# Early distance tables, other places for the dilated tiles, later forget sums and one held gate tile in a hybrid attention layer

## The chip, the cores and the metric

The kernel runs on one core of a Trainium2 chip. It is one launch of a whole decoder layer in float32. The metric is the device time of that launch in microseconds; lower is better. The kernel was run three times and profiled in one more execution.

## What the reference computes

One layer over x of 1024 positions by 1024 channels. Cut to what matters here:

```python
h = rms_norm(x, norm_mix_g)
proj = h @ w_in      # 3*768 dilated q,k,v | 3*512 forgetting q,k,v | 8 forget | 2*1024 gates
for g, (window, dilation) in enumerate(((128, 1), (512, 4), (2048, 16))):
    # 4 heads of 64 each: query t sees t, t-d, ..., t-window, with an ALiBi slope
    outs[g], lses[g] = dilated_window_attention(q[g], k[g], v[g], window, dilation, slopes[g])
o_a = sum(softmax(lses, over g) * outs)              # 256 channels
o_b = forgetting_attention(q, k, v, log_sigmoid(f_logit))   # 8 heads, causal, 512 channels
#   logit[t, s] = q_t.k_s/8 + c_t - c_s, c = cumsum of the log forget gates
x = x + (sigmoid(gate_a) * (o_a @ w_dil_out) + sigmoid(gate_b) * (o_b @ w_fox_out)) @ w_out
h2 = rms_norm(x, norm_ffn_g)
x = x + (silu(h2 @ w_g) * (h2 @ w_u)) @ w_ffn_down    # 2816 hidden channels
return rms_norm(x, norm_final_g)
```

## The kernel before

**How queues are ordered.** The kernel is written as one Python function, and a list scheduler of the framework orders the instructions of every engine when it is built, by a simulated time line; on the chip every engine then works through its queue in that order and waits on semaphores. A pool of tiles takes a place in SBUF when it is opened; a later pool may lie over bytes that an earlier one has given back. An instruction that writes such a tile waits on the chip for the last readers and writers of just those bytes (`reuse_waits="tile"`).

**Arithmetic.** A float32 matmul is made of three: `split` (L94 to 96) takes a tensor apart into a rounded high part, a copy on ScalarE, and the rest, a subtraction on VectorE; `mm3` (L98 to 101) then issues high by high, low by high and high by low. On the profile's rows such groups have the tiles `wh`, `wl` and the like.

**Stages, by their time in the profile.** To about 66 us the input is normed and transposed to `hT`, and the values of the forgetting attention are made. Then come the values of the dilated attention (pool `dilv`, to 140 us): eight row tiles by `w0` (264 columns, the last eight of which are the forget logits `lf`) and eight by `w12` (512 columns), stored by ScalarE's DMA queue to `vd_dram`. `form` (L393 to 418), called twice, makes the tables T1 to T4, sums of quarters of `hT` for a fast block product (seven products in place of eight). The pool `cums` (L451 to 485) makes the running sums of the log forget gates: a triangular matrix `upper` on POOL (GpSimd), a chain of logarithms on VectorE and ScalarE, two matmuls, and the small tile `negc`, which is a bias of the first attention's scores. From there to 270 us, `projections` (L275 to 310) makes q and k of the forgetting attention and four dilated ones, two column tiles in a call, eight calls in all; its weight sums s12 and s34 are made on POOL by `left_side` (L254 to 266). Then the forgetting attention (`fox_qk`, `fox_scores`, `fox_exp`, `fox_values`; 270 to 511 us) and the dilated one (`dil_qk`, `dil_scores`, `dil_exp`, `dil_values`; to 673 us). Both go in units: scores of one unit, then the values of the one before. Each unit has a maximum over partitions on POOL (`partition_all_reduce`).

**Filler.** Two lists are multiplied by `ahead` (L214 to 225) whenever the scheduler finds room on TensorE during both attentions: BESIDE, the eight other tiles of dilated q and k, and `merge_order`, the sixteen tiles of gate logits. One such tile is 48 matmuls of 512 columns into two banks `pf`, two copies by ScalarE into a tile `fst` (two buffers), and a store on ScalarE's DMA queue to `dqk_dram` or `g_dram`. Their pool `ahead` lies on the right side of SBUF, over bytes of the projections' pool (`cc`, `v2`, `v3`).

**Around the dilated attention.** Its pool `dil` holds three distance tables R0 to R2 (L617 to 645; two IOTAs, masks on POOL and VectorE, scratch in the pool `dilm`), then the values `vd` in one tile of 24,576 bytes per partition (three loads on POOL's queue, L647 to 650), then the pool `dila`: six dqk tiles of 4,096 bytes (loads on SP's queue), score tiles L0, L1, L2, the maxima Mx, and `o`. All of it begins at the end of `hT`, at bytes that T and then `vf`, `ql`, `qx`, `kx` and `qraw` of the first attention have held. The scratch of the tables has the bytes 28,160 to 32,256 from there, and so has the first dqk tile.

**Merge.** From 684 us the pool `gates`, at the same first bytes, loads the attention outputs from `o_dram` to `land` tiles (POOL's queue), splits them to `oh` and `ol` (`oh` of the first branch: the first 16,384 bytes), multiplies by the output weights and by the sigmoid of the gates read from `g_dram`. Then follow w_out, the feed-forward's first half (to 1264 us) and second half.

## Time and profile before

| | |
|---|---|
| median of the runs | 1544.46 us (1544.28 to 1544.62) |
| profiled execution, its own time | 1544.29 us |
| span of its instructions | 1542.5 us |
| TensorE clock granted, mean | 0.987 of full speed |
| busy: TensorE, its weight loads, VectorE, ScalarE, GpSimd | 96%, 78%, 58%, 35%, 27% |
| moved by DMA | 171.62 MB, mean 111 GB/s |

Times in the rows are microseconds from the start of the span. PE is TensorE, PEld its weight loads, DVE VectorE, ACT ScalarE, POOL GpSimd, SP SyncE; a name with a q, as SPq, is the part of an engine that issues DMAs. A row names the line, the operation and its tiles as output<-input, with the numbers of buffers left out. The busy time of an engine does not count waiting.

### The profile page before, as it was taken

What the parts mean: (1) busy time and instruction counts of PE and PEld (TensorE: products, weight loads), DVE (VectorE), ACT (ScalarE), POOL (GpSimd) and SP (SyncE); (2) the same over time, 40 slices, a digit from 0 to 9 for tenths busy, and PEclk for the clock granted to TensorE, in tenths of its full rate; (3) what the DMA queues carried; (4) which work ended last, traced back from release to release, by engine and by line L of the source; (5) the groups of instructions that cost most, each with busy time, mean ns of one, the idle gap of its engine ahead of it and who ended that gap; (6) DMA issues with size and microseconds to landing.
All of it is one profiled execution on the core that took longest, in us unless ns stands there. A gap on an engine that the chain in (4) does not pass through costs nothing.

```text
span 1542.5 us, 18138 instructions
## 1 busy us (share of the span) xinstructions
PE 1478.9 (96%) x6956; PEld 1196.4 (78%) x6956; DVE 895.5 (58%) x1321; ACT 536.0 (35%) x808; POOL 419.1 (27%) x351
## 2 busy tenths in 40 slices
PE   7998999799999999979999999999999999999997
PEld 6898888676767777758888778888878877788886
DVE  6741433299997289846727864444444445956546
ACT  5321222376665123335414332222222224312113
POOL 1001331263452111100000145555555553140000
PEclk9999999999999999989999999999999999999999
DMA  7231333743332651145713122222222225642302
GB/s 219 71 101 48 95 109 110 218 109 106 99 103 69 209 181 55 55 163 185 265 56 136 42 69 82 82 82 82 83 82 82 82 88 195 204 140 82 96 15 96
DMA packets 139047, 171.62 MB, mean 111 GB/s; under 512 B 6992, under 2 KB 108368, under 8 KB 138960
## 3 DMA queue, kind: packets, MB, share of 16 engines
q1 hardware_dynamic: 119824, 112.25, 24.4%
q0 software_dynamic: 9616, 34.62, 6.1%
q10 hardware_dynamic: 9520, 23.60, 4.1%
q8 instruction: 55, 0.90, 0.2%
q14 instruction: 32, 0.26, 0.1%
HBM read 123.25 MB, written 47.19 MB: 110 GB/s over the span
## 4 chain that ended last, share of the span: by engine, by line
PE 79%; DMA 6%; DVE 4%; POOL 4%; ACT 3%; issue 2%; SPq 1%; ACTq 0%; POOLq 0%; DVEq 0%
PE pd L272 25%; PE pd L100 10%; PE pd L101 10%; PE pd L99 10%; PE pf L101 4%; PE pf L100 4%; PE pf L99 4%; DMA wr<-in_w_ffn_in_dram 2%; ACT wh L95 2%; PE pd L189 2%; PE pd L190 2%; PE pd L193 2%; PE pd L589 2%; POOL sg L969 1%; DVE wl L96 1%
## 5 line engine op out<-in xcount | busy, mean ns | idle before, releaser
L95 ACT ACTIVATE wh<-wr 128x1024 fp32r<-128x1024 f32 (+2 forms) x152 | 140.6, 932 | 342.8 <-PE pd L100 92.7
L96 DVE TENSOR_TENSOR wl<-wr,wh 128x1024 fp32r<-128x1024 f32 (+2 forms) x152 | 166.9, 1102 | 143.7 <-ACT wh L95 143.4
L272 PE MATMUL pd<-hT_t,wh 128*128 128x512 f32 x784 | 244.7, 393 | 3.0 <-ACT c L952 2.3
L272 PE MATMUL pd<-tT,wh 128*128 128x512 f32 x672 | 206.4, 389 | 0.9 <-DVE v L884 0.6
L272 PEld LDWEIGHTS pd<-hT_t,wh 128*128 128x128 f32 x784 | 148.3, 190 | 34.5 <-ACT c L952 2.7
L99 PE MATMUL pf<-hT_t,wh 128*128 128x512 f32 x384 | 151.7, 395 | 8.0 <-ACT fst L224 7.8
L272 PE MATMUL pd<-hT_t,wl 128*128 128x512 f32 x392 | 155.0, 396 | 1.5 <-DVE wl L96 1.1
L100 PE MATMUL pf<-hT_t,wh 128*128 128x512 f32 x384 | 151.9, 396 | 0.0
L101 PE MATMUL pf<-hT_t,wl 128*128 128x512 f32 x384 | 151.6, 395 | 0.0
L272 PEld LDWEIGHTS pd<-tT,wh 128*128 128x128 f32 x672 | 126.0, 188 | 27.9 <-DVE v L884 1.1
L99 PE MATMUL pd<-wh,wh 128*128 128x512 f32 x352 | 137.4, 391 | 4.4 <-DVE acc L1012 3.1
L100 PE MATMUL pd<-wl,wh 128*128 128x512 f32 x352 | 137.0, 389 | 0.0
L101 PE MATMUL pd<-wh,wl 128*128 128x512 f32 x352 | 137.0, 389 | 0.0
L272 PE MATMUL pd<-tT,wl 128*128 128x512 f32 x336 | 129.7, 389 | 0.2 <-DVE wl L96 0.2
L1012 DVE TENSOR_TENSOR acc<-pd,acc 128x512 f32<-128x512 f32 x128 | 85.8, 688 | 68.2 <-PE pd L101 68.1
L259 POOL TENSOR_TENSOR s<-wr 128x512 f32<-128x512 f32 x26 | 36.6, 1409 | 293.7 <-DVE tT L96 192.4
L96 DVE TENSOR_TENSOR wl<-s,wh 128x1024 fp32r<-128x1024 f32 x52 | 64.8, 1246 | 67.8 <-ACT wh L95 67.8
L95 ACT ACTIVATE wh<-s 128x1024 fp32r<-128x1024 f32 x52 | 55.1, 1060 | 131.4 <-POOL s L260 98.4
L99 PEld LDWEIGHTS pf<-hT_t,wh 128*128 128x128 f32 x384 | 72.5, 189 | 27.1 <-ACT fst L224 9.2
L272 PEld LDWEIGHTS pd<-hT_t,wl 128*128 128x128 f32 x392 | 74.4, 190 | 22.4 <-DVE wl L96 7.1
L101 PEld LDWEIGHTS pf<-hT_t,wl 128*128 128x128 f32 x384 | 72.5, 189 | 20.0 <-issue 5.7
L100 PEld LDWEIGHTS pf<-hT_t,wh 128*128 128x128 f32 x384 | 72.5, 189 | 19.0 <-issue 4.2
(220 smaller groups left out, 2781.4 us busy)
## 6 DMA issues: line engine op xcount, KB each, us to landing
wr<-in_w_in_dram SPq DMA_DIRECT2D x46, 512.0 KB, 4.3
wr<-in_w_ffn_in_dram SPq DMA_DIRECT2D x44, 512.0 KB, 4.3
wr<-a_dram SPq DMA_DIRECT2D x22, 512.0 KB, 4.3
wr<-in_w_ffn_down_dram SPq DMA_DIRECT2D x22, 512.0 KB, 4.0
a_dram<-a POOLq DMA_DIRECT2D x20, 512.0 KB, 4.9
qraw<-fqk_dram SPq DMA_DIRECT2D x32, 256.0 KB, 4.1
g_dram<-fst ACTq DMA_DIRECT2D x16, 512.0 KB, 2.7
land<-g_dram SPq DMA_DIRECT2D x16, 512.0 KB, 3.4
```

The source lines that it names most:

```text
L95: nc.scalar.activation(out=hi, in_=src, func=AF.Copy)
L96: nc.vector.tensor_tensor(out=lo, in0=src, in1=hi.bitcast(F32), op=ALU.subtract)
L99: nc.tensor.matmul(psum, w.hi, m.hi, start=start, stop=False)
L100: nc.tensor.matmul(psum, w.hi, m.lo, start=False, stop=False)
L101: last_mm[0] = nc.tensor.matmul(psum, w.lo, m.hi, start=False, stop=stop)
L189: nc.tensor.matmul(pt[hh][:], w.hi[:, k], m.hi, start=(k == 0), stop=False)
L190: nc.tensor.matmul(pt[hh][:], w.hi[:, k], m.lo, start=False, stop=False)
L193: nc.tensor.matmul(pt[hh][:], w.lo[:, k], m.hi, start=False, stop=(k == kt - 1))
L259: nc.gpsimd.tensor_tensor(out=s12[:, :4], in0=u1, in1=u2, op=ALU.add)
L272: last_mm[0] = nc.tensor.matmul(bank[:], p, q, start=first and k == 0 and n == 0, stop=k == 3 and n == 2, skip_group_check=True)
L589: nc.tensor.matmul(po[half[e], HALF - width[j]:], vf[:, j, pr, e], L[:, off[j]:off[j + 1]], start=(j == nj - 1), stop=(j == 0), skip_group ...
L1012: nc.vector.tensor_tensor(out=acc[:, t, cs], in0=pt[:], in1=acc[:, t, cs], op=ALU.add)
```

## The change

- `split` returns its VectorE instruction, and the two calls of `form` are put under `tc.issue_after` the last split of the value weights: the scheduler issues nothing of them before it.
- The pool `cums` becomes a function `decay`, called in the pool of the projections after the first two calls of `projections`.
- The filler's pool moves from the right side to the left, to the end of `hT`, and holds R0 to R2 as well, which are made there before the first attention's pool opens. Per partition it has 3,584 bytes of tables and then two `fst` of 4,096 bytes. The scratch `dilm` now lies over the first bytes of `vf`.
- `vd` becomes three tiles. Two are loaded in the pool `dil`, the third in `dila` after the first scores. `o` is allocated after the first scores of a pair of heads, and the score tiles in the order L0, L2, Mx, L1.
- The last of the sixteen gate tiles is put under `tc.issue_after` the last value matmul of the dilated attention.

```diff
--- before.py
+++ after.py
@@ -93,7 +93,7 @@
 
     def split(hi, lo, src):
         nc.scalar.activation(out=hi, in_=src, func=AF.Copy)
-        nc.vector.tensor_tensor(out=lo, in0=src, in1=hi.bitcast(F32), op=ALU.subtract)
+        return nc.vector.tensor_tensor(out=lo, in0=src, in1=hi.bitcast(F32), op=ALU.subtract)
 
     def mm3(psum, w, m, start, stop):
         nc.tensor.matmul(psum, w.hi, m.hi, start=start, stop=False)
@@ -429,7 +429,7 @@
                 for c0, n, at in cols:
                     raw = wpool.tile([P, KT, n], F32, tag="wr" if n == P else "wf", name=nm("wr"), bufs=2 if n == P else 1)
                     nc.sync.dma_start(out=raw[:], in_=w_in[:, c0:c0 + n].rearrange("(k p) c -> p k c", p=P))
-                    split(w.hi[:, :, at:at + n], w.lo[:, :, at:at + n], raw[:])
+                    last = split(w.hi[:, :, at:at + n], w.lo[:, :, at:at + n], raw[:])
             for g0, w, n in ((0, w0, 264), (1, w12, 512)):
                 for tt in range(NT):
                     pv = pd()
@@ -445,10 +445,12 @@
                     else:
                         nc.scalar.dma_start(out=vd_dram[1:3, tt].rearrange("g p c -> p g c"),
                                             in_=st[:].rearrange("p (g c) -> p g c", g=2))
-            form(0)
-            form(2)
-
-        with pool_of("cums", 1) as cums:
+            with tc.issue_after(last.ins):
+                form(0)
+                form(2)
+
+        def decay(cums):
+
             upper = cums.tile([P, P], F32, name="upper", bufs=1)
             nc.gpsimd.memset(upper[:], 1.0)
             nc.gpsimd.affine_select(out=upper[:], in_=upper[:], compare_op=ALU.is_ge, fill=0.0, base=0,
@@ -490,12 +492,44 @@
                 for a in range(2):
                     c0 = FOX0 + a * FOX_W + pr * P
                     projections(upool, T, (c0, c0 + P), [fqk_dram[a, pr + i] for i in range(2)], (1, 1), 1.0)
+                if pr == 0:
+                    decay(upool)
             for two in TWOS:
                 projections(upool, T, [dil_cols(*t) for t in two], [dqk_dram[t] for t in two],
                             [STR[a][g] for u, g, a in two], (SCALE, 1.0)[two[0][2]])
 
-    f_ctx = pool_of("ahead", 1, side="right")
+    f_ctx = pool_of("beside", 1)
     fpool = f_ctx.__enter__()
+
+    R0 = fpool.tile([P, 256], F32, name="R0", bufs=1)
+    R1 = fpool.tile([P, 2, 256], F32, name="R1", bufs=1)
+    R2 = fpool.tile([P, P], F32, name="R2", bufs=1)
+    with pool_of("dilm", 1) as mpool:
+        ri = mpool.tile([P, 256], I32, name="ri", bufs=1)
+        nc.gpsimd.iota(out=ri[:], pattern=[[1, 256]], base=0, channel_multiplier=-1)
+        nc.vector.tensor_copy(R0[:], ri[:])
+        nc.vector.tensor_scalar(out=R2[:], in0=R0[:, :P], scalar1=8.0, scalar2=None, op0=ALU.mult)
+        nc.gpsimd.affine_select(out=R0[:], in_=R0[:], compare_op=ALU.is_ge, fill=BIG, base=0,
+                                pattern=[[1, 256]], channel_multiplier=-1)
+        nc.gpsimd.affine_select(out=R0[:], in_=R0[:], compare_op=ALU.is_ge, fill=BIG, base=P,
+                                pattern=[[-1, 256]], channel_multiplier=1)
+        nc.gpsimd.affine_select(out=R2[:], in_=R2[:], compare_op=ALU.is_ge, fill=BIG, base=0,
+                                pattern=[[1, P]], channel_multiplier=-1)
+
+        odd = mpool.tile([P, P], I32, name="odd", bufs=1)
+        oddf = mpool.tile([P, P], F32, name="oddf", bufs=1)
+        nc.vector.tensor_scalar(out=odd[:], in0=ri[:, :P], scalar1=1, scalar2=None, op0=ALU.bitwise_and)
+        nc.vector.tensor_copy(oddf[:], odd[:])
+        nc.vector.scalar_tensor_tensor(out=R2[:], in0=oddf[:], scalar=BIG, in1=R2[:],
+                                       op0=ALU.mult, op1=ALU.add)
+
+        r1 = mpool.tile([P, 2, 256], I32, name="r1", bufs=1)
+        nc.gpsimd.iota(out=r1[:], pattern=[[-1, 2], [1, 256]], base=0, channel_multiplier=-2)
+        nc.vector.tensor_copy(R1[:], r1[:])
+        nc.gpsimd.affine_select(out=R1[:], in_=R1[:], compare_op=ALU.is_ge, fill=BIG, base=0,
+                                pattern=[[-1, 2], [1, 256]], channel_multiplier=-2)
+        nc.gpsimd.affine_select(out=R1[:], in_=R1[:], compare_op=ALU.is_ge, fill=BIG, base=P,
+                                pattern=[[1, 2], [-1, 256]], channel_multiplier=2)
 
 
     with pool_of("fox", 1) as spool:
@@ -613,41 +647,15 @@
 
 
     with pool_of("dil", 1) as spool:
-
-        R0 = spool.tile([P, 256], F32, name="R0", bufs=1)
-        R1 = spool.tile([P, 2, 256], F32, name="R1", bufs=1)
-        R2 = spool.tile([P, P], F32, name="R2", bufs=1)
-        with pool_of("dilm", 1) as mpool:
...
-        vd = spool.tile([P, 3, NT, 2, 2, DH], F32, name="vd", bufs=1)
-        for g in range(3):
-            nc.gpsimd.dma_start(out=vd[:, g].rearrange("p t a b d -> p t (a b d)"),
+        vd, last_pv = [None, None, None], [None]
+
+        def load_vd(pool, g):
+            vd[g] = pool.tile([P, NT, 2, 2, DH], F32, tag=f"vd{g}", name=nm("vd"), bufs=1)
+            nc.gpsimd.dma_start(out=vd[g][:].rearrange("p t a b d -> p t (a b d)"),
                                 in_=vd_dram[g].rearrange("t p c -> p t c"))
+
+        load_vd(spool, 0)
+        load_vd(spool, 1)
 
         def dil_qk(pool, u):
 
@@ -662,9 +670,9 @@
 
 
 
-            L0, L1, L2, Mx = [[pool.tile([P] + d, F32, tag=n, name=nm(n), bufs=bufs) for e in range(2)]
-                              for n, d, bufs in (("L0", [NT, P], 3), ("L1", [2, 2, 256], 3),
-                                                 ("L2", [4, P], 3), ("Mx", [HALF], 4))]
+            L0, L2, Mx, L1 = [[pool.tile([P] + d, F32, tag=n, name=nm(n), bufs=bufs) for e in range(2)]
+                              for n, d, bufs in (("L0", [NT, P], 3), ("L2", [4, P], 3),
+                                                 ("Mx", [HALF], 4), ("L1", [2, 2, 256], 3))]
 
             def rows(g, a, e):
                 return qk[g][a][half[e]]
@@ -758,8 +766,8 @@
             for i in range(n):
                 for e, one in zip((1, 0), todo):
                     dst, g, tt, src = one[i]
-                    nc.tensor.matmul(dst, vd[:, g, tt, u, e], src, start=(i == 0), stop=(i == n - 1),
-                                     skip_group_check=True)
+                    last_pv[0] = nc.tensor.matmul(dst, vd[g][:, tt, u, e], src, start=(i == 0), stop=(i == n - 1),
+                                                  skip_group_check=True)
             for e in (1, 0):
                 nc.tensor.matmul(den[half[e], :], ones[:, :64], scs[e][3][:], start=True, stop=True)
             finish(pool, po, den, o[:, b::2])
@@ -770,17 +778,23 @@
             pend = None
             for u in range(2):
                 qk = dil_qk(apool, u)
-                o = apool.tile([P, S], F32, tag="o", name=nm("o"), bufs=1)
                 for b in range(2):
-                    unit = dil_scores(apool, qk, u, b), u, b, o
+                    scs = dil_scores(apool, qk, u, b)
+                    if b == 0:
+                        o = apool.tile([P, S], F32, tag="o", name=nm("o"), bufs=1)
+                    if not pend:
+                        load_vd(apool, 2)
+                    unit = scs, u, b, o
                     if pend:
                         dil_values(apool, *pend)
                     pend = unit
             dil_values(apool, *pend)
 
-    for br, dt in merge_order:
+    for i, (br, dt) in enumerate(merge_order):
         n = br * KT + dt
-        ahead(fpool, GATE0 + n * P, g_dram[n])
+
+        with tc.issue_after(last_pv[0].ins) if i == 2 * KT - 1 else ExitStack():
+            ahead(fpool, GATE0 + n * P, g_dram[n])
     f_ctx.__exit__(None, None, None)
```

## Rows read from the trace of the kernel before

**Rows 1.** Page, part 1: busy us (share) xinstructions.

```profile
PE 1478.9 (96%) x6956; PEld 1196.4 (78%) x6956; DVE 895.5 (58%) x1321; ACT 536.0 (35%) x808; POOL 419.1 (27%) x351
```

**Rows 2.** Timeline, PE, idle time before a row and its releaser bracketed.

```profile
70.05 0.39 PE L100 MATMUL pd<-wv,hT_t 128*128 128x264 f32 x1 [2.02 <-DVE wv L96]
...
143.65 0.41 PE L475 MATMUL pd<-lf,upper 128*128 128x64 f32 x2 [3.63 <-DVE lf L471]
...
149.36 0.73 PE L272 MATMUL pd<-hT_t,wh 128*128 128x512 f32 x2 [0.69 <-ACT cc L285]
...
274.51 0.50 PE L99 MATMUL pf<-hT_t,wh 128*128 128x512 f32 x1 [1.47 <-ACT fst L224]
...
292.06 0.79 PE L99 MATMUL pf<-hT_t,wh 128*128 128x512 f32 x1 [6.38 <-ACT fst L224]
...
539.70 3.27 PE L338 MATMUL pd<-dqk,dqk 64*128 64x128 f32 x32 [2.03 <-DMA dqk<-dqk_dram]
...
544.88 2.89 PE L338 MATMUL pd<-dqk,dqk 64*128 64x128 f32 x32 [0.71 <-DMA dqk<-dqk_dram]
...
684.50 2.07 PE L189 MATMUL pd<-oh,wh 128*128 128x512 f32 x4 [11.31 <-ACT oh L95]
```

**Rows 3.** Windows: stretch, us, five engines' busy us, granted clock, DMA share, GB/s.

```profile
278.00:282.00 4.00, 4.00 (x19) 3.30 (x19) 0.00 (x0) 0.75 (x1) 0.00 (x0) 1.00 1.02 343
...
290.00:294.00 4.00, 1.94 (x5) 1.47 (x6) 1.97 (x2) 3.38 (x4) 0.00 (x0) 0.63 0.19 54
294.00:298.00 4.00, 4.00 (x14) 3.46 (x13) 3.24 (x6) 2.31 (x6) 1.61 (x4) 0.52 0.94 260
...
505.00:510.00 5.00, 5.00 (x24) 3.49 (x21) 2.69 (x4) 2.78 (x4) 0.00 (x0) 1.00 0.07 26
...
540.00:545.00 5.00, 4.29 (x37) 3.68 (x35) 3.53 (x10) 0.00 (x0) 0.00 (x0) 0.66 0.94 324
...
684.00:690.00 6.00, 5.50 (x13) 4.34 (x14) 4.81 (x4) 4.54 (x5) 1.07 (x2) 0.50 0.68 248
```

**Rows 4.** Line L400: ns min/median/max, first to last start us.

```profile
L400 DVE TENSOR_TENSOR f<-f,f x8: 1216/1219/1227, 60.1 to 90.5; 128x1024 f32<-128x1024 f32 x8
```

**Rows 5.** Timeline, POOL and PE, 140 to 160 us.

```profile
147.71 1.27 POOL L259 TENSOR_TENSOR s<-wr 128x512 f32<-128x512 f32 x1 [7.06 <-issue]
...
152.62 1.20 PE L272 MATMUL pd<-tT,wh 128*128 128x512 f32 x4 [0.25 <-ACT wh L95]
```

**Rows 6.** Line L259, columns as in rows 4.

```profile
L259 POOLq MODIFY_POOL_CONFIG  x4: 11/24/37, 140.7 to 689.0; - x4
```

**Rows 7.** Chain that ended last: start us, us, what.

```profile
153.97 91.88 PE pd L272 x404
```

**Rows 8.** Timeline, POOL and SP, 505 to 545 us.

```profile
519.27 0.34 POOL L622 IOTA ri<- 128x256 int32 x1 [8.01 <-PE pf L101]
...
524.46 7.20 SPq L658 DMA_DIRECT2D dqk<-dqk_dram  x6
```

**Rows 9.** Tile vf, 265 to 345 us, columns as in rows 4.

```profile
L589 PE MATMUL pd<-L,vf x16: 272/432/592, 322.1 to 323.9; 128*64 128x128 f32 x4, 128*64 128x256 f32 x4, 128*64 128x384 f32 x4, 128*64 128x512 f32 x4
L503 POOL DMA_DIRECT2D vf<-vf_dram x1: 929/929/929, 270.6 to 270.6; - x1
...
DMA to landing us min/median/max: 15.6/15.6/15.6
```

**Rows 10.** Timeline, ACT, 268 to 295 us.

```profile
290.47 1.06 ACT L514 ACTIVATE kx<-qraw 128x1024 fp32r<-128x1024 f32 x1 [4.27 <-DMA qraw<-fqk_dram]
```

**Rows 11.** Timeline, POOL and ACT, 672 to 690 us.

```profile
677.37 1.12 POOL L799 DMA_DIRECT2D land<-o_dram  x2
...
683.39 2.14 ACT L95 ACTIVATE oh<-land 128x1024 fp32r<-128x1024 f32 x2 [8.77 <-DMA land<-o_dram]
```

**Rows 12.** Tile fst, 480 to 720 us.

```profile
L224 ACT ACTIVATE fst<-pf x24: 575/579/601, 484.4 to 674.0; 128x512 f32<-128x512 f32 x24
...
DMA to landing us min/median/max: 2.6/2.9/7.2
```

More of the change, by code (lines that the diff above doesn't have):

```diff
@@ L615, in layer_kernel @@
     with pool_of("dil", 1) as spool:
-        R0 = spool.tile([P, 256], F32, name="R0", bufs=1)
-        R1 = spool.tile([P, 2, 256], F32, name="R1", bufs=1)
-        R2 = spool.tile([P, P], F32, name="R2", bufs=1)
-        with pool_of("dilm", 1) as mpool:
-            ri = mpool.tile([P, 256], I32, name="ri", bufs=1)
-            nc.gpsimd.iota(out=ri[:], pattern=[[1, 256]], base=0, channel_multiplier=-1)
-            nc.vector.tensor_copy(R0[:], ri[:])
-            nc.vector.tensor_scalar(out=R2[:], in0=R0[:, :P], scalar1=8.0, scalar2=None, op0=ALU.mult)
-            nc.gpsimd.affine_select(out=R0[:], in_=R0[:], compare_op=ALU.is_ge, fill=BIG, base=0,
-                                    pattern=[[1, 256]], channel_multiplier=-1)
-            nc.gpsimd.affine_select(out=R0[:], in_=R0[:], compare_op=ALU.is_ge, fill=BIG, base=P,
-                                    pattern=[[-1, 256]], channel_multiplier=1)
-            nc.gpsimd.affine_select(out=R2[:], in_=R2[:], compare_op=ALU.is_ge, fill=BIG, base=0,
-                                    pattern=[[1, P]], channel_multiplier=-1)
-            odd = mpool.tile([P, P], I32, name="odd", bufs=1)
-            oddf = mpool.tile([P, P], F32, name="oddf", bufs=1)
-            nc.vector.tensor_scalar(out=odd[:], in0=ri[:, :P], scalar1=1, scalar2=None, op0=ALU.bitwise_and)
-            nc.vector.tensor_copy(oddf[:], odd[:])
-            nc.vector.scalar_tensor_tensor(out=R2[:], in0=oddf[:], scalar=BIG, in1=R2[:],
-                                           op0=ALU.mult, op1=ALU.add)
-            r1 = mpool.tile([P, 2, 256], I32, name="r1", bufs=1)
-            nc.gpsimd.iota(out=r1[:], pattern=[[-1, 2], [1, 256]], base=0, channel_multiplier=-2)
-            nc.vector.tensor_copy(R1[:], r1[:])
-            nc.gpsimd.affine_select(out=R1[:], in_=R1[:], compare_op=ALU.is_ge, fill=BIG, base=0,
-                                    pattern=[[-1, 2], [1, 256]], channel_multiplier=-2)
-            nc.gpsimd.affine_select(out=R1[:], in_=R1[:], compare_op=ALU.is_ge, fill=BIG, base=P,
-                                    pattern=[[1, 2], [-1, 256]], channel_multiplier=2)
```

## Prediction

> **What bounds the kernel now.** I read the page's busy times first: TensorE is busy for 1478.9 of 1542.5 us [rows 1], so what a change can win is its idle time and the stretches in which its clock is low. Next I went through TensorE's timeline for idle times of 0.3 us and more; the eight up to 700 us that matter here are in [rows 2], each with what ended it: 2.02 us on a VectorE split, 3.63 us on the forget sums, 0.69 us on a copy, 1.47 and 6.38 us on ScalarE's evacuation of a filler bank, 2.03 and 0.71 us on the loads of the dilated q and k, 11.31 us on the split of the attention output before the merge. Then the windows [rows 3], for the granted clock: after 6.38 us of idling it is 0.63 and 0.52 in the next two 4 us, and 0.50 (the 1.2 GHz level) for the 6 us after the 11.31 us.
>
> The filler is what makes this a sum of idle times. The 24 tiles of `ahead` (eight BESIDE, sixteen gates, 48 matmuls each) are put by the scheduler wherever TensorE would otherwise stand through both attentions. All of them must run anyway. So up to the merge, time is TensorE's work plus its idle time, as long as filler is left; where none is left, the chain of the attention itself sets it.
>
> **Tables of the fast product (`form`).** Its 24 VectorE operations (8 each of sums, differences and splits; 1.22 us each [rows 4]) now queue behind the last split of `w12`. In before the sums run from 60.1 to 90.5, some of them ahead of the split of `w0` that kept TensorE 2.02 us until 70.05. That goes: -2.0 us. Even if all 24 began only at 90.5, they would be done after 29.3 us of VectorE, at 120, and the first product that reads the tables stands at 152.62 [rows 5]: cover of 30 us, so nothing is added. Bounds 0 and -2.3.
>
> **Forget sums.** After the last `w12` matmul (143.65 - 3.63 = 140.0 us) before does two things in a row. TensorE idles those 3.63 us for the logarithm chain, because the sums are first in line. And on POOL the `upper` memset, which lies over `w12`'s bytes and waits for it, stands ahead of a MODIFY_POOL_CONFIG (first at 140.7 [rows 6]); the first `s12` sum starts only 7.06 us later, at 147.71. So the first product of a combined weight is at 152.62. With `decay` behind the first pair of projections, that configuration is the next thing on POOL after the last store of values and is over long before, and `s12` waits for `w12` alone: from 140.0, three sums of 1.27 us and a copy of 1.1 us give 144.9. TensorE's own work before it is 24 matmuls of 91.88/404 = 0.227 us [rows 7] and the 0.69 us wait for a copy: 140.0 + 5.5 + 0.7 = 146.2, which is later and so decides. 152.6 - 146.2 = 6.4 us, less 0.4 us for the two matmuls of the sums (0.41 in the row of 143.65), which run later: -6.0 us. The sums' 4 us on VectorE then lie beside the projections and nobody needs them before the first scores, more than 100 us later. If the schedule still put `upper` ahead of `s12`, POOL's 7.06 us would stay and the term would be 0; at best it is -7.
>
> The page GPSIMD Engine Reference of the Trainium skill (section Instruction dispatch) puts the first call after such a reload at about 5.95 us. This trace has 7.06 us here and up to 8.01 us at the IOTA [rows 8]. By the page's figure `s12` would have started at 146.6 and the term would be -4.9; the rows decide.
>
> **Distance tables early.** R0 to R2 are made when T falls free (about 270, where `vf` starts) instead of at 519 to 524. IOTA and the projections' sums share a configuration, so I expect no reload there; of VectorE and POOL they need the 5.2 us from the IOTA (519.27) to the first dqk load (524.46) at most, and VectorE does nothing from 278 to 282 [rows 3]. What is queued behind them is `vf`, whose bytes now lie over the tables' scratch: its load, at 270.6 before, moves to about 276. It took 15.6 us to land and its first reader is at 322.1 [rows 9], so 30 us are spare. But the loads of q and k (`qraw`) get the transfer engines first. They are saturated there (share 1.02), k is waited for until 290.47 [rows 10], and the filler's evacuation stands behind that wait on ScalarE: the 6.38 us. With 2 MB starting 5 us later q lands some 5 us sooner, its two buffers come free, and k follows. The filler's `fst` no longer lies over the projections' `v3`, so the 1.47 us should go as well. All there is to win: 1.47 + 6.38 + clock 4 x 0.37 + 4 x 0.48 = 11.3 us. Nothing in before shows how the two loads share, so the bounds are 0 and -11; I take -5, the time by which the load is put off.
>
> **Dilated tiles over what frees first.** In before the first dqk tile lies exactly over the tables' scratch (both start 28,160 bytes after `hT_t`, 4,096 long), so the loads stand behind IOTA (8.01 us after POOL's previous work ended, at 511.3) and the whole table chain, and start at 524.46. Adding up the tile sizes after the change, vd0 and vd1 lie on `vf`, the six dqk on `ql`, `qx`, `kx`, L0 and L2 on `qraw` and the short L, Mx on Mx. All of those have had their last reader well before the attention's last store, so the dqk loads can go once the schedule reaches them, which I put just behind the last store of the first attention, near 511: 13 us sooner. vd0 and vd1 can load from 505, where the transfer engines are idle (share 0.07). The 2.03 and 0.71 us and a clock of 0.66 for 5 us (1.7 us) are there to win, 4.4 in all; I take -4, bounds 0 and -5.
>
> **One gate tile held.** Its 48 matmuls, 48 x 0.227 = 10.9 us, now come after the last value product. The 11.31 us wait ran from 673.2 to 684.5: the loads of the attention outputs stand at 677.37 on POOL's queue, their split at 683.39 [rows 11]. So 10.9 us nearly fill it. But `fst` now lies at bytes 3,584 to 11,776 after `hT_t`, and the merge's `oh` takes bytes 0 to 16,384 there: its first split must wait for the store of the held tile. From the held tile's last matmul on, evacuation 0.6, store to landing 2.9 [rows 12], split 1.1. Idle 4.6 us in place of 11.3: -6.7 us. The clock still falls (0.63 stood behind the idling of 6.38). Bounds: -11.3 - 3 (no wait, clock kept for the 6 us at 0.50) and +4.2 (third rival).
>
> Does filler last? The dilated chain took 539.7 to 673.2 = 133.5 us. Started 13 us sooner, at 526.7, it ends at 660.2; with the held tile and 4.6 us the merge starts at 675.7 (in before's time); by work and idle time it starts at 684.5 - 4 - 6.7 = 673.8. The two meet within 2 us, so the terms stand, with nothing to spare.
>
> **Sum.** -2.0 - 6.0 - 5 - 4 - 6.7 = -23.7 from the profiled execution's 1544.3 us: 1520.6; the median of the runs is 0.2 above that execution, so 1521.
>
> **Rivals.**
> 1. *The q and k loads gain nothing.* The bytes are the same and the engines are full from 278 to 282; k then lands when it did. For it: the share of 1.02. Against: in that stretch vf is not needed and q is. Time 1521 + 5 = 1526, chance 0.17. The Trainium skill (Trainium Kernel Development and Optimization, Key Constraints) says that loads of all queues run on the same 16 engines and interleave; by that this rival holds unless order matters.
> 2. *The configuration stays in front of `s12`*, behind `upper`: the 6.0 us are lost, 1527. For it: nothing but the scheduler's freedom. Chance 0.08.
> 3. *Filler runs short.* If the dqk loads still start near 524, the chain ends at 673, the held tile is only added behind it, and the merge starts at 673.2 + 10.9 + 4.6 = 688.7: +4.2 against 684.5 in place of -10.7, 1536 in all. Chance 0.08.
> 4. *The merge's wait is covered whole*, because the first split does not meet `fst`: the 4.6 us and 6 x 0.5 = 3 us of clock more, 1513. Chance 0.08.
> 5. *Slower:* the tables have no reader before 524. If the schedule queues the IOTAs behind the first all-reduce, which needs k (290.47), its scores and their masks, say at 305 (an estimate), POOL changes configuration twice more (8 and 6 us), `vf` is issued near 318 and lands past 334, after its reader at 322, and all-reduces stand behind. It costs more than it gains once values wait 25 us, that is when `vf` lands after 347; then 1547 to 1555. Against it: they are first in program order and free at 270. Chance 0.06.
> 6. *No change:* the gains come back as waits elsewhere in a new order of all queues; 1543 to 1546. Chance 0.05.
>
> My forecast keeps 0.48. What a measurement tells from no change is 0.2%, 3 us. Faster: 0.48 + 0.17 + 3 x 0.08 = 0.89; same 0.05; slower 0.06. The range reaches over rivals 1 to 4, 1512 to 1536.
>
> **What would show it.** Right: no idle time of TensorE at 67 to 70; tT products from 146; POOL's first `s12` sum within 1 us of `w12`'s end; vf issued after q; no reload between the attentions; dqk loads near 500 in the new time; an `oh` split that waits for g_dram's store, 5 us of idling. Wrong: a first `s12` 7 us late; k landing no sooner; TensorE idle inside the dilated stage; a merge wait of 10 us or none.

## The result, and the profile after

The median of four runs is 1530.93 us (1528.89 to 1534.02) after 1544.37 us; ratio 0.9915, 95% interval 0.9896 to 0.9934. That is 13.4 us faster where 23 were forecast. The total is inside the range, but its terms did not come as they were worked out: one came to nothing, one to two thirds of its size, one to twice its size, and a loss that the prediction had weighed and set aside took 11.6 us back.

The page of the changed kernel, part 1 (busy us, share of the span, instructions):

```profile
PE 1472.8 (96%) x6956; PEld 1191.4 (78%) x6956; DVE 893.3 (59%) x1321; ACT 537.0 (35%) x808; POOL 418.9 (27%) x351
```

The work is the same, instruction for instruction on TensorE; its span is 1527.0 us. What answers to [rows 2] is TensorE's timeline, idle time in brackets with what ended it:

```profile
70.09 0.39 PE L100 MATMUL pd<-wv,hT_t 128*128 128x264 f32 x1 [2.01 <-DVE wv L96]
...
143.48 0.74 PE L272 MATMUL pd<-hT_t,wh 128*128 128x512 f32 x2 [0.69 <-ACT cc L285]
...
148.62 1.19 PE L272 MATMUL pd<-tT,wh 128*128 128x512 f32 x4 [2.13 <-ACT wh L95]
...
543.42 0.70 PE L338 MATMUL pd<-dqk,dqk 64*128 64x256 f32 x2 [1.44 <-DVE L L689]
...
648.24 6.77 PE L769 MATMUL pd<-L,vd 128*64 128x256 f32 x64 [9.21 <-ACT L L745]
...
672.43 2.08 PE L189 MATMUL pd<-oh,wh 128*128 128x512 f32 x4 [5.45 <-ACT oh L95]
```

There are four things to see here. The 2.02 us near 70 have stayed. The 3.63 us for the forget sums have gone, with 2.13 us in their place; the first product of a combined weight comes at 148.62 instead of 152.62. (That this is 4.0 us and not the 1.5 between the two waits is mostly the clock, see the last row below.) The 1.47 and 6.38 us of the first attention's start and the 2.03 and 0.71 us of the dilated loads have gone. And there is a new wait of 9.21 us, for the exponentials of the last dilated unit: there is no filler left for it. The wait of the merge fell from 11.31 to 5.45 us.

The windows that answer to [rows 3] (stretch, us, busy time of PE, PEld, DVE, ACT, POOL with instructions, granted clock, DMA share, GB/s):

```profile
290.00:294.00 4.00, 4.00 (x19) 3.33 (x18) 2.84 (x3) 2.82 (x4) 0.00 (x0) 1.00 0.33 90
294.00:298.00 4.00, 4.00 (x22) 3.47 (x21) 1.85 (x4) 2.64 (x6) 1.64 (x5) 1.00 0.99 274
...
648.00:652.00 4.00, 3.77 (x20) 2.25 (x22) 2.48 (x3) 0.18 (x1) 0.00 (x0) 0.50 0.00 0
652.00:656.00 4.00, 4.00 (x53) 3.19 (x50) 0.00 (x0) 0.08 (x1) 0.00 (x0) 0.88 0.00 0
...
672.00:676.00 4.00, 3.57 (x8) 2.82 (x9) 3.59 (x4) 3.22 (x4) 0.53 (x1) 0.50 0.33 102
...
888.00:892.00 4.00, 4.00 (x19) 3.31 (x18) 2.19 (x3) 2.03 (x3) 0.00 (x0) 1.00 0.93 259
```

The clock that was 0.63 and 0.52 behind the 6.38 us is now 1.00; it falls to 0.50 behind the new 9.21 us instead. One row of the kernel before, behind its 3.63 us:

```profile
144.00:148.00 4.00, 4.00 (x13) 3.21 (x13) 2.08 (x10) 0.00 (x0) 0.29 (x1) 0.57 0.00 0
```

There the low clock cost another 4.00 x 0.43 = 1.7 us; behind the 2.13 us of the changed kernel it stays at 1.00.

Lost clock is counted as the busy time of a window times what is missing to 1. With that the sum closes: forget sums -4.0 (their clock included); first attention -7.85 of idling and 1.94 x 0.37 + 4 x 0.48 = 2.6 of clock, -10.5; dilated loads -2.74, +0.92 for the wait at 543, and 4.29 x 0.34 = 1.5 of clock, -3.3; the new wait 9.21 + 3.77 x 0.50 + 4 x 0.12 = +11.6; the merge's wait -5.9, and -0.8 from the merge's start to the transposition named next, mostly its clock. Together -12.9 us. The transposition that waits 0.98 us after the merge, in both kernels, stands at 846.04 in place of 858.93: -12.9. The rest of this profile's gain (15.5 us of span) lies after the merge and is in the main clock behind short waits, which changes from execution to execution (e8).

**Where q and k wait now.** ScalarE's timeline from 262 to 300 us (it answers to [rows 10]), and below it SP's and POOL's:

```profile
266.80 1.09 ACT L224 ACTIVATE fst<-pf 128x512 f32<-128x512 f32 x2 [1.84 <-PE pd L272]
...
280.17 1.06 ACT L95 ACTIVATE wh<-wr 128x1024 fp32r<-128x1024 f32 x1 [4.62 <-PE pf L100]
281.14 0.58 ACT L224 ACTIVATE fst<-pf 128x512 f32<-128x512 f32 x1
...
282.19 2.02 ACT L548 ACTIVATE qx<-qraw 128x1024 fp32r<-128x1024 f32 x2 [0.47 <-ACT fst L224]
...
291.29 1.06 ACT L548 ACTIVATE kx<-qraw 128x1024 fp32r<-128x1024 f32 x1 [0.95 <-DMA qraw<-fqk_dram]
```

```profile
266.79 2.68 SPq L547 DMA_DIRECT2D qraw<-fqk_dram  x4
...
284.53 10.18 SPq L547 DMA_DIRECT2D qraw<-fqk_dram  x8
```

```profile
271.29 0.93 POOL L537 DMA_DIRECT2D vf<-vf_dram  x1
...
511.59 0.57 POOL L629 DMA_DIRECT2D o_dram<-o  x1 [3.11 <-DVE o L329]
```

As forecast, vf is issued 4.5 us behind q. But k comes no sooner, at 291.29 (the last copy of k began at 292.16 in the kernel before). ScalarE now evacuates the filler at once, and its copies of q stand behind a weight copy that waits for filler (280.17), though the four loads of q took only 4.6 to 7.3 us from issue to landing; the buffers of q come free late, and k's loads go at 284.53. So the order on ScalarE has turned around: in before the filler waited for k, now q waits for the filler. TensorE is busy all the while, with filler: 131 matmuls of it from 255 to 295 us, in place of 75 in the kernel before from 259 to 299, where the same work stands 4 us later. The last store of the first attention is issued by 512.2 (511.59 + 0.57); before, POOL's work ahead of the IOTA ended at 511.3 [rows 8], and that was this store. It is no earlier, though some 12 us ahead of it (4.0 of the forget sums, 7.85 of idling) are gone.

### The profile page after: what moved, and what is told of

It is laid out like the page before. It is cut to its first block, busy times and chain, and to the rows that moved or that the text cites. A ratio compares the mean times of both kernels' runs of the same rounds, so it can differ in the third digit from the quotient of the medians.

```text
span 1527.0 us, 18124 instructions
## 1 busy us (share of the span) xinstructions
PE 1472.8 (96%) x6956; PEld 1191.4 (78%) x6956; DVE 893.3 (59%) x1321; ACT 537.0 (35%) x808; POOL 418.9 (27%) x351
## 4 chain that ended last, share of the span: by engine, by line
PE 83%; DMA 4%; DVE 4%; ACT 4%; POOL 3%; issue 2%; SPq 0%; ACTq 0%; POOLq 0%; DVEq 0%
PE pd L272 25%; PE pd L101 10%; PE pd L100 10%; PE pd L99 10%; PE pf L99 5%; PE pf L101 5%; PE pf L100 5%; DMA wr<-in_w_ffn_in_dram 2%; PE pd L623 2%; ACT wh L95 2%; PE pd L189 2%; PE pd L190 2%; PE pd L193 2%; POOL sg L983 1%; PE pd L769 1%
## 5 line engine op out<-in xcount | busy, mean ns | idle before, releaser
L259 POOL TENSOR_TENSOR s<-wr 128x512 f32<-128x512 f32 x26 | 41.0, 1575 | 358.1 <-DMA wr<-in_w_ffn_in_dram 260.5
```

Source lines behind the costliest of these rows:

```text
L259: nc.gpsimd.tensor_tensor(out=s12[:, :4], in0=u1, in1=u2, op=ALU.add)
```

## Experiments

All times are medians of four to six runs, each set beside eleven of the kernel before on the same chip; the ratio is to those. Every stage time is from the run's own profile.

**e1: no held tile**

```diff
-        with tc.issue_after(last_pv[0].ins) if i == 2 * KT - 1 else ExitStack():
-            ahead(fpool, GATE0 + n * P, g_dram[n])
+        ahead(fpool, GATE0 + n * P, g_dram[n])
```

> The changed kernel with the last gate tile no longer held. Theory A (filler runs out before the last value products, so the held tile is missing there): the 9.21 us that TensorE idled before them at 648.24 are mostly filled, the wait before the merge goes from 5.45 back to about 11.3 us, the first product of the merge comes at about 668 in place of 672.4, and the time falls by about 4 us, to 1526 to 1528. Theory B (the prediction: the held tile only shortens the wait before the merge): the 5.9 us come back, 1537.

1526.01 us, ratio 0.9891 (0.9874 to 0.9908). TensorE's timeline:

```profile
669.97 2.07 PE L189 MATMUL pd<-oh,wh 128*128 128x512 f32 x4 [11.28 <-ACT oh L95]
```

No idle time near 650; the merge waits 11.28 us and yet starts 2.5 us sooner. That is less than the forecast 4 because this execution had lost 1.7 us early on, behind the 2.13 us wait near 148, where the changed kernel's profile has a full clock:

```profile
150.00:154.00 4.00, 4.00 (x13) 3.08 (x11) 3.25 (x2) 2.18 (x3) 1.62 (x1) 0.57 0.21 51
```

Without that it is 4.2 us. Theory A in every step. In the changed kernel the held tile did not pay: what it saved at the merge was missing in the chain.

**e2: tables of the fast product where they were**

```diff
-            with tc.issue_after(last.ins):
-                form(0)
-                form(2)
+            form(0)
+            form(2)
```

> The changed kernel with form free to be issued before the last split, as before. Theory A (the split of w0 stands behind the copy of the last bank of first-attention values on VectorE, and form has no part in its wait): idle time of TensorE near 70 us stays 2.0 us, the time is that of the changed kernel within 1.5 us. Theory B (the prediction: form ahead of the split costs 2.0 us, now hidden by something else that form would add to): 2 us slower.

1533.77 us, ratio 0.9942 (0.9926 to 0.9958). The wait near 70 us is 2.02 us, and the last value products stand at 648.24, to the hundredth where they were. So `form` has no part in that wait. Whether it is worth anything is not settled: the intervals overlap, and 1533.77 stands beside 1530.93 and 1532.67 (e8) of the changed kernel. VectorE's timeline of the changed kernel shows what the split waits for:

```profile
66.94 0.69 DVE L378 COPY vst<-pd 128x512 f32<-128x512 f32 x1 [4.75 <-PE pd L101]
67.55 2.48 DVE L96 TENSOR_TENSOR wv<-wr,wv 128x1024 fp32r<-128x1024 f32 x3
```

It stands in the queue behind the copy of the last bank of values, and VectorE was idle for 4.75 us before that copy.

**e3: forget sums in front of the projections again**

```diff
-                if pr == 0:
-                    decay(upool)
+        with pool_of("cums", 1) as cums:
+            decay(cums)
```

> The changed kernel with the forget sums in front of the projections, as before. Theory A (POOL's configuration behind upper and the logarithm chain set the first combined product): that product is back at 152 to 153 from 148.6, idle 3.6 us for the chain and the clock falls behind it; 4 to 6 us slower, 1535 to 1537. Theory B (the scheduler makes it good with filler later): under 1.5 us.

1534.62 us, ratio 0.9945 (0.9929 to 0.9961). The 3.63 us are back, and the merge starts at 675.94, 3.5 us later than in the changed kernel, about what the first combined product lost (3.7, from 148.62 to 152.35). Theory A by stage; of the time, 2 to 4 us, with the spread of the runs as large as that.

**e4: oh no longer over fst**

```diff
+        m0 = mpool.tile([P, S], F32, tag="m", name=nm("m"), bufs=LAG + 2)
         load_o(1, 2, 4)
...
-                ms[dt] = mpool.tile([P, S], F32, tag="m", name=nm("m"), bufs=LAG + 2)
+                ms[dt] = mpool.tile([P, S], F32, tag="m", name=nm("m"), bufs=LAG + 2) if dt else m0
```

> The changed kernel with the merge's first tile m allocated ahead of oh, so that oh no longer lies over the filler's fst. Theory A (the first split waits for the store of the held tile): TensorE's idle time before the merge falls from 5.45 to about 1 us, the clock no longer falls behind it, and the time falls by 4.5 to 7 us, to 1524 to 1526. Theory B (the loads of the attention outputs, issued from 660.3 on and landing in up to 7.7 us, end as late): under 1.5 us of difference.

1527.35 us, ratio 0.9908 (0.9886 to 0.9930). ScalarE's first copies of the merge, first in the changed kernel, then here:

```profile
671.32 3.90 ACT L95 ACTIVATE oh<-land 128x1024 fp32r<-128x1024 f32 x4 [3.41 <-DMA g_dram<-fst]
```

```profile
668.25 3.90 ACT L95 ACTIVATE oh<-land 128x1024 fp32r<-128x1024 f32 x4 [0.48 <-DMA land<-o_dram]
```

The releaser is the answer: the store of the held tile, and without the overlap the loads of the attention output. The copies come 3.1 us sooner and TensorE's wait is 2.52 us. So the collision that the prediction worked out from the addresses is there, at 3 us. Theory A has the cause; its time, 1524 to 1526, was missed, and with single runs at 1532 and 1534 the ratio's interval overlaps that of the changed kernel.

**e5: fst on the right again, tables early on the left**

```diff
-    f_ctx = pool_of("beside", 1)
-    fpool = f_ctx.__enter__()
+    r_ctx = pool_of("beside", 1)
+    rpool = r_ctx.__enter__()
+    f_ctx = pool_of("ahead", 1, side="right")
+    fpool = f_ctx.__enter__()
...
-    R0 = fpool.tile([P, 256], F32, name="R0", bufs=1)
+    R0 = rpool.tile([P, 256], F32, name="R0", bufs=1)
...
```

> The changed kernel with the filler's two fst tiles back on the right side of SBUF, over the projections' bytes; the tables stay early on the left, and everything of the dilated attention moves 8,192 bytes down. Theory A (it is the new place of fst that lets ScalarE evacuate the filler ahead of the q and k copies): the idle times of 1.5 and about 6.4 us near 274 and 292 are back, with the low clock behind them; the first attention ends about 10 us later, but the filler that was not used there fills the 9.21 us before the last value products, and fst is no longer under oh, so that little of it is left in the end: 1526 to 1532. Theory B (the prediction: the tables put vf off, and q and k come sooner): both idle times stay away, the 9.21 us stay, the wait before the merge falls by 2 to 3 us as in the kernel with oh off fst; 1526.

1519.79 us, ratio 0.9840 (0.9827 to 0.9854): 12.9 us faster than the changed kernel beside it (1532.67, e8), the fastest version here. Its rows of TensorE, ScalarE, SP and POOL:

```profile
644.73 6.15 PE L771 MATMUL pd<-L,vd 128*64 128x256 f32 x64 [1.92 <-ACT L L747]
...
664.28 1.20 PE L189 MATMUL pd<-oh,wh 128*128 128x512 f32 x4 [1.44 <-ACT oh L95]
```

```profile
269.85 1.09 ACT L224 ACTIVATE fst<-pf 128x512 f32<-128x512 f32 x2 [5.34 <-DVE qo L290]
...
272.17 1.06 ACT L550 ACTIVATE qx<-qraw 128x1024 fp32r<-128x1024 f32 x1 [1.23 <-DMA qraw<-fqk_dram]
```

```profile
266.34 20.79 SPq L549 DMA_DIRECT2D qraw<-fqk_dram  x10
```

```profile
504.12 0.57 POOL L631 DMA_DIRECT2D o_dram<-o  x1 [3.24 <-DVE o L329]
```

Both theories are wrong in part. The 1.47 us came back, as A had it; the 6.38 us did not (the first scores behind them wait 1.56 us), as B had it. And what neither had: q's first copy starts at 272.17 and not at 282.19, the first attention ends 7.5 us sooner, and so the filler lasts: 1.92 us of idling before the last value products in place of 9.21. The filler in the stretch from 255 to 295 (busy us, matmuls, clock, DMA share, GB/s), in the changed kernel and here:

```profile
255.00:295.00 40.00, 30.18 (x131) 1.00 0.67 211
```

```profile
255.00:295.00 40.00, 24.34 (x103) 1.00 0.76 221
```

**e6: distance tables late again (fst stays on the left)**

```diff
-    R0 = fpool.tile([P, 256], F32, name="R0", bufs=1)
...
     with pool_of("dil", 1) as spool:
+        R0 = spool.tile([P, 256], F32, name="R0", bufs=1)
...
```

> The changed kernel with R0 to R2 made again at the start of the dilated attention, inside its pool; fst stays on the left. Theory A (fst's place freed the filler's evacuation, the tables only free the start of the dilated attention): no idle time near 274 and 292; POOL changes its configuration again before the IOTAs (about 8 us), the loads of dilated q and k stand behind the tables, and the first dilated scores come 8 to 13 us later than 524.5; with the filler then short, 1536 to 1543. Theory B (the tables early are what put vf off and q and k ahead): 6 us of idling are back near 292.

1538.48 us, ratio 0.9957 (0.9943 to 0.9970), 5.8 us slower than e8 beside it. TensorE:

```profile
534.84 3.35 PE L338 MATMUL pd<-dqk,dqk 64*128 64x128 f32 x32 [3.92 <-DMA dqk<-dqk_dram]
...
658.29 1.97 PE L769 MATMUL pd<-L,vd 128*64 128x256 f32 x8 [13.51 <-ACT L L745]
```

Theory A: nothing comes back near 292, the dilated scores start 10.4 us later, their loads at 520.5 behind IOTAs that waited 7.02 us, and the chain waits 13.51 us at its end.

**e7: dilated tiles in their old places**

```diff
-        load_vd(spool, 0)
-        load_vd(spool, 1)
+        for g in range(3):
+            load_vd(spool, g)
...
-            L0, L2, Mx, L1 = [[pool.tile([P] + d, F32, tag=n, name=nm(n), bufs=bufs) for e in range(2)]
+            L0, L1, L2, Mx = [[pool.tile([P] + d, F32, tag=n, name=nm(n), bufs=bufs) for e in range(2)]
...
```

> The changed kernel with all three vd tiles in the pool of the dilated attention, the score tiles in their old order and o allocated ahead of the scores. Theory A (the dilated tiles' place sets when their loads go, once the tables are early): the first loads of dilated q and k move from 500.5 to 511 or later, the first dilated scores by some 5 to 10 us, and since the chain of the dilated attention now sets the end, the time rises by as much. Theory B (the early tables alone freed the loads): the loads stay near 500, the time within 2 us.

1533.58 us, ratio 0.9926 (0.9912 to 0.9940), 0.9 us above e8. The loads of the dilated q and k (ns min/median/max, first to last start):

```profile
L666 SPq DMA_DIRECT2D dqk<-dqk_dram x12: 338/423/547, 500.1 to 559.2; - x12
```

They start at 500.1; in the changed kernel at 500.5. Theory B: the early tables alone freed the loads. The merge starts 1.8 us later than in the changed kernel (674.27), and the time is 0.9 us longer; the new places are worth 1 to 2 us or nothing.

**e8: the changed kernel once more**

> The changed kernel itself once more, beside the three others on the same chip. Both theories: the order of every queue is the same, so idle times up to the merge agree with the first profile within 0.2 us each; where its time differs, it is by the clock granted behind the short waits after the merge, which was full behind the waits at 848 and 887 us in the first profile and 0.63 to 0.82 at the same places in the profile of the kernel before.

1532.67 us, ratio 0.9916 (0.9902 to 0.9930). Every wait up to 887 us is within 0.1 us of the first profile's (9.88 us at the very start: 10.22), yet the span is 3.0 us longer. The window behind a wait of 2.37 us, to be set beside the row of 888 above:

```profile
888.00:892.00 4.00, 4.00 (x12) 3.14 (x11) 1.21 (x2) 0.78 (x2) 0.00 (x0) 0.57 0.93 257
```

Twelve matmuls in place of nineteen, after the same wait: 7 x 0.227 = 1.6 us of the 3.0. The rest came in steps of 0.3 to 0.6 us in the feed-forward, at a granted clock of 1.00 in both profiles, where the expectation had all of it by the clock.

**e9: e5 without the held tile** (the edit of e1 on top of e5's)

> The kernel of e5 (fst on the right) with the last gate tile no longer held. Theory A (a held tile pays where the filler lasts to the last value products, which it nearly does here: 1.92 us of idling): the 1.92 us go, the wait before the merge goes from 1.44 back to about 11.3 us and the clock falls behind it; the merge starts at about 664.3 + 11.3 - 1.4 - 1.9 = 672, the time rises by 8 to 11 us, 1528 to 1531. Theory B (the held tile costs wherever it is, as in e1): some 4 us less, 1516.

1522.37 us, ratio 0.9877 (0.9859 to 0.9896). TensorE:

```profile
667.28 2.08 PE L189 MATMUL pd<-oh,wh 128*128 128x512 f32 x4 [8.03 <-ACT oh L95]
```

The merge starts 3.0 us later than in e5 and the time is 2.6 us above; by the ratios, each to the kernel before on its own chip, it is 0.0037 or 5.7 us. (Each of the two profiles lost 1.7 us of clock ahead of the merge where the other did not: here it was 0.57 from 150 to 154 us, in e5 0.66 from 535 to 540.) Direction as A, size not: some filler still stood behind the last value products, so the wait came back to 8.03 and not to 11.3 us. With e1 it shows that the held tile changes its sign with the filler: 2.5 us lost at the merge (4.2 without the clock lost early in e1) where 9.21 us of filler were missing, 3.0 us won where 1.92 were.

**e10: the held tile alone, on the kernel before**

```diff
+        with tc.issue_after(last_pv[0].ins) if i == 2 * KT - 1 else ExitStack():
+            ahead(fpool, GATE0 + n * P, g_dram[n])
```

> The kernel before with the last gate tile held and nothing else changed; fst is on the right there, so not under oh. Theory A (the dilated chain has little slack: from first scores to last value products it took 133.5 us in the kernel before and 130.5 us in the changed one, where 9.21 us of it were idle): holding 10.9 us of filler leaves about 8 us of idling in the chain, ends it about 3 us sooner, and the wait before the merge falls from 11.31 to about 1 us; the merge starts 2 to 3 us sooner, and with the clock, low once more in the chain but no longer behind the merge's wait, the time falls by 2 to 5 us, to 1539 to 1542. Theory B (the prediction's sum of idle times): 10 us and the clock, 1531.

1537.28 us, ratio 0.9960 (0.9947 to 0.9974): 6.2 us. TensorE:

```profile
665.40 5.93 PE L763 MATMUL pd<-L,vd 128*64 128x256 f32 x64 [5.65 <-ACT L L739]
...
684.73 1.20 PE L189 MATMUL pd<-oh,wh 128*128 128x512 f32 x4 [1.44 <-ACT oh L95]
```

Of the 9.9 us won in the wait of the merge 5.65 came back in the chain. The merge starts no earlier than in [rows 2] because this execution was 2.4 us behind by 146 us (most of it by low clock behind the wait near 70); so it is some 2 us there, as A had it. The time is 1.7 us better than A's bound and 6 short of B's.

**e11: e5 with the forget sums meant to come later**

```diff
                 if pr == 0:
-                    decay(upool)
+                    with tc.issue_after(last_mm[0].ins):
+                        decay(upool)
```

> The kernel of e5 with the forget sums also put under issue_after the last product of the first pair of projections. Theory A (in the changed kernel the copy of s12 at 147.53 stands in ScalarE's queue behind the logarithm of the sums, though POOL had s12 ready at 144.1): TensorE's 2.12 us at 148 go, the first combined product comes at about 146, and the time falls by 2 us, to 1517.5. Theory B (POOL or the weights set it): 2.1 us stay, no difference.

1533.99 us, ratio 0.9944 (0.9923 to 0.9964), 14 us above e5. The edit did not do what was meant: named after a matmul, `issue_after` held only the instructions of TensorE. The two matmuls of the sums moved from 160.5 to 184.8 us, the logarithm chain of the other engines stayed where it was, and so did the 2.12 us. The question of the 2.13 us is not answered. But the scheduler's order changed further on, and that run is a second test of the loads. POOL, SP, ScalarE and TensorE:

```profile
272.91 0.93 POOL L540 DMA_DIRECT2D vf<-vf_dram  x1
```

```profile
275.15 24.77 SPq L550 DMA_DIRECT2D qraw<-fqk_dram  x10
```

```profile
289.42 1.06 ACT L551 ACTIVATE qx<-qraw 128x1024 fp32r<-128x1024 f32 x1 [15.07 <-DMA qraw<-fqk_dram]
```

```profile
291.02 0.79 PE L99 MATMUL pf<-hT_t,wh 128*128 128x512 f32 x1 [5.92 <-ACT fst L224]
```

Here vf is issued 2.2 us ahead of q, and the loads of q take 10.8 to 13.4 us to land. q's first copy starts 14.3 us after the issue of its load, and the wait of the filler behind it, 5.92 us, is back, with the tables early and fst on the right.

**e12: the early tables alone, on the kernel before**

```diff
+    r_ctx = pool_of("beside", 1)
+    rpool = r_ctx.__enter__()
...
+    R0 = rpool.tile([P, 256], F32, name="R0", bufs=1)
...
     with pool_of("dil", 1) as spool:
-        R0 = spool.tile([P, 256], F32, name="R0", bufs=1)
...
```

> The kernel before with R0 to R2 made early in a pool of their own on the left and nothing else changed; fst stays on the right. Theory A (the early tables put vf off behind q, and free the start of the dilated attention of the IOTAs and their change of configuration): q lands about 5 us sooner after the issue of its load than in before (10.9 us there), the 6.38 us near 292 fall to about 1.5, the 1.47 us stay, the loads of dilated q and k start 8 to 13 us sooner and the 2.03 and 0.71 us near 540 go; with the clock 10 to 14 us faster, 1531 to 1535. Theory B (fst's place was needed for the first attention): the 6.38 us stay, 4 to 5 us faster, 1540.

1529.53 us, ratio 0.9911 (0.9894 to 0.9927): this one part gives what the whole change gives (0.9915). SP, POOL and ScalarE:

```profile
272.90 20.90 SPq L546 DMA_DIRECT2D qraw<-fqk_dram  x10
```

```profile
277.40 0.93 POOL L536 DMA_DIRECT2D vf<-vf_dram  x1
```

```profile
278.85 1.06 ACT L547 ACTIVATE qx<-qraw 128x1024 fp32r<-128x1024 f32 x1 [1.35 <-DMA qraw<-fqk_dram]
```

With vf 4.5 us behind q, q's first copy starts 6.0 us after the issue of its load; before, with vf 0.3 us behind, 10.9 us (270.36 to 281.25). The filler's 6.38 us are gone (the first scores wait 1.3), the 1.47 stay, the dilated loads start at 497.8 and nothing waits for them. Theory A, at 1.5 us below its range.

## Why the prediction came out as it did

**Tables of the product, -2.0: nothing.** The step that failed is that sums ahead of the split kept it back. They stand ahead of it again in e2, and the wait is the same; the split's place is behind the copy of the last bank. Whether `form` is worth anything elsewhere e2 leaves open.

**Forget sums, -6.0: -4.0.** The mechanism was right. The change of configuration comes at 68.5 us, over 70 us ahead of its use, POOL's first `s12` sum starts as soon as `w12` is done, and TensorE has its 24 matmuls. Mis-sized is what decides after that: not TensorE's own work (146.5) but the copy of s12 on ScalarE. In the changed kernel:

```profile
147.37 0.26 ACT L471 ACTIVATE u<-u 128x64 f32<-128x64 f32 x1 [2.67 <-DVE t L469]
147.53 1.04 ACT L95 ACTIVATE wh<-s 128x1024 fp32r<-128x1024 f32 x1
```

POOL had s12 ready at 144.1. The copy stands behind a logarithm of the sums, which the scheduler had brought forward again. That the 2.13 us are due to it is read from these rows and was not tested, since e11 did not move the chain.

**Distance tables early, -5: by far the largest.** Alone 14.0 us (e12, 1543.49 to 1529.53). The step on the loads was right, and of rival 1 the premise, that q gains nothing, is out: vf 4.5 us behind q took q's copy from 10.9 to 6.0 us after issue (e12), vf 2.2 us ahead of it made it 14.3 (e11). In the changed kernel itself k came no sooner, which the prediction had named as a sign of being wrong; the loads were not to blame but the copies on ScalarE. That loads of all queues interleave on the same engines, as the Trainium skill says (Trainium Kernel Development and Optimization, Key Constraints), agrees with this: with vf 0.3 us behind the first of them, the four loads of q took 5.2 to 12.9 us to land in the kernel before, and 4.8 to 7.0 in e12, where vf came later. By that alone order would not matter; here it did, by 5 us in one direction and 3 in the other. The size was off twice: all of the 6.38 us and the clock behind them went with 5 us, and the start of the dilated loads, which the prediction gave to the tiles, belongs here too (e6, e7).

**Dilated tiles, -4: 1 to 2 us or nothing.** The waits and the low clock of that place are gone, but they go with the old places as well (e7). The step that failed gave to the new places what the early tables do by themselves: with no tables made there, neither IOTA's change of configuration nor the overlap with their scratch stands ahead of the loads, which start at 497.8 in e12 in the old places.

**One gate tile held, -6.7: -5.9 of waiting at the merge, and more than that lost elsewhere.** The wait for the store of the held tile was right (e4), its size too (5.45 us for 4.6). But the step that carries it failed: *does filler last*. It compared the dilated chain with TensorE's work and found them 2 us apart. It put the chain's start at 526.7 in the time of the kernel before, as if the first attention ended sooner by all the 13 us that had been gained ahead of it. In fact the scores started at 524.49 in the new time. The first attention ended when it had ended before, at 511.59: q waited for filler, and 56 more filler matmuls had gone into the 40 us around its start. The filler from the first dilated scores to the merge (columns as in e5), in the kernel before, in the changed kernel and in e5:

```profile
539.70:684.50 144.80, 86.93 (x347) 0.96 0.31 105
```

```profile
524.49:672.43 147.94, 85.06 (x343) 0.96 0.28 93
```

```profile
517.67:664.28 146.61, 95.50 (x381) 0.98 0.29 95
```

So no more filler was left for the chain than before, where a start 13 us sooner would have left some 57 more (13 / 0.227, an estimate), and 48 of the 343 were held back: 10.9 us, against 9.21 us of idling. In e5, with 38 more, 1.92 us are left of it. TensorE idle inside the dilated stage was the prediction's own sign of being wrong. Rival 3 was worked out for a late start of the loads; it came by this road instead, while the loads were early.

**What the prediction didn't cost.** It took fst's move to the left for the price of one wait at the merge and a gain of 1.47 us at 274. With fst back on the right, e5 is 12.9 us faster than e8. In the profiles its merge starts 8.2 us sooner: 4.0 us are the merge's wait (5.45 to 1.44), most of it the collision that the prediction had; not costed were the 7.3 us in the chain (9.21 to 1.92), against which 3.0 us of waiting come back at the first attention's start. The rest of the 12.9 us lies after the merge and in the spread of the runs. On the left the filler's first evacuation waits 1.84 us for a product of the projections, on the right 5.34 us for their last combination on VectorE; with the earlier place the schedule has more filler ahead of q. Rivals 2, 4, 5 and 6 did not come; the IOTAs that rival 5 put behind an all-reduce stand at 266.8, ahead of vf.

So the total came inside the range in part by luck: some 9 us too little for the distance tables (with the dilated loads counted to them) stood against some 8 too much for the tiles, the product's tables and the sums together and the 11.6 us of missing filler. The forecast itself was 10 us off.

## What to carry to other kernels

Where idle time is filled with spare work, a wait removed early is worth only what it brings forward the chain that comes after; follow the chain's start, not the sum of waits, and count how much filler is left at its end. A place in memory that lets spare work start sooner is not free: it decides what stands in front of the critical copies in the same queue. Holding work back to cover a wait pays only while nothing on the way goes short of it; in two layouts of one kernel the same edit won some 3 us at the merge and lost 2.5 to 4.

## What the runs showed of the hardware

For two transfers on two queues the moment of issue decided: q's first copy, which needs two of its loads, started 10.9 us after their issue with vf (2 MB) issued 0.3 us behind, 6.0 with vf 4.5 us behind (e12), and 14.3 with vf 2.2 us ahead (e11). vf itself took 15.6, 16.8 and 12.4 us to land. And the clock behind a short wait is not fixed: after 2.4 us of idling TensorE's granted clock stayed at 1.00 in one execution and was 0.57 for the next 4 us in another, with the same queues; after 2.0 us near 70 it was 1.00 from 70 to 74 us in the kernel before and 0.63 in e10, whose edit comes later; after 1.45 us near 535 it was 0.66 from 535 to 540 us in e5. The four runs of the changed kernel show it too: the two near 1529 us had a mean clock of 0.992, those at 1532 and 1534 us 0.988 and 0.989. How much of that spread of 5 us it makes is not shown; between the two profiles it is 1.6 of 3.0 us.
